# The second layer's output projection, all columns by seven block products, with the weight sums made in HBM

## The chip, the cores and the metric

One core of a Trainium2 chip. The metric is the device time of one launch in microseconds (us), as the median of runs; the kernel before has 2065.95 us (three runs, 2065.65 to 2066.11). TensorE is PE in the profile, VectorE DVE, ScalarE ACT, GpSimd POOL, SyncE SP. SP and POOL, and ACT for stores, issue the DMAs.

## The reference

A decoder trunk of two layers on x (1 x 512 x 2048, float32): a gated differential attention and a gated RWKV-7 time mixing. Each layer is a norm, a wide input projection, a mixer, a gate and an output projection that is added to x. The change concerns the last line of the second layer:

```
def rwkv7_mixer(h, ...):
    p = h @ w_in                          # 2048 -> 4*2048 + 192
    p = p + (token_shift(p) - p) * mu
    ...
    y = wkv7_scan(rh, heads(decay), kh, vh, -kk, kk * ah)     # 32 heads of 64, 512 tokens
    ...
    y = y.reshape(B, T, RW_WIDTH).astype(h.dtype) * jax.nn.silu(g)
    return y @ w_out                      # (512 x 2048) @ (2048 x 2048)

x = x + out
```

## The kernel before, in words

**Precision.** Every large matmul is made of three (`mm3`, L118): each float32 operand is split into a high and a low part, and high x high, high x low and low x high are summed in PSUM. The high part of a weight is a cast on ACT (L109), the low part a difference on DVE (L110), both in `split_w`. In the first layer's heads the same two stand at L615 and L616. A step is a stationary tile of 128 x 128 and 512 moving columns.

**Weights.** `w_out` lies as four column blocks of 512, each 16 K tiles of 128 rows. A load takes two K tiles (128 x 2 x 512 floats, 0.524 MB) from SP's queue into one of three buffers `wraw`; the split goes into four buffers `wh` and four `wl`, each one K tile.

**First layer.** Two dense units of 192 matmuls (`unit_tok`, 16 K tiles x 4 row tiles x 3), each with eight loads by L76 on SP, then seven heads by block products, whose weights are summed while loading: a second load of POOL's queue is added to a first one in SBUF (L588, `accum_op`).

**Second layer.** 16 rounds, one for each pair of heads. A round has four projections of 48 matmuls (`unit_chan`), with two loads each; a list of hooks (`behind`) hangs further work after the matmuls of certain K tiles. The scan of the pair before (`scan_pair`), cut into small steps, is spread between the matmuls. Each round's gated row of y (128 x 512) is stored to HBM (`yd2`). The last two rows stay in SBUF.

**The output projection** (end of `layer1`): the rows of y come back from HBM by `Feed` and are split (`split_row`). Column blocks 0 and 1 are dense units; the first runs beside the last scan, whose end is forced ahead of the last K tile (`all_rows`). Column blocks 2 and 3 go together through `seven`: the first 12 K tiles are two halves of 6, the 512 tokens two halves of 256, the 1024 columns two halves of 512. Seven block products, named 11, 12, 22, S1 to S4, stand for the eight; the last four K tiles are plain. A block product is 3 loads x 2 K tiles x 2 row tiles x 3 = 36 matmuls, a plain load 24. The sums of y (S1 to S4) are made by `sum_forms` on DVE and ACT during the second dense unit; the sums of the weights are added to blocks in SBUF by POOL (L790). Results are added to x by DVE (L827) and stored by ACT.

**What sets the order.** A scheduler orders each engine's instructions by priority and by their dependences. `issue_after(ins)` puts what it wraps behind `ins`, for the instructions on the engine of `ins`; `add_manual_dep` and priorities are the other means. Engines and DMA queues then run their instructions in the order built, each waiting on semaphores.

Of the kernel before, what the change touches and what calls it, by code (L numbers as in the profile page):

```python
# [13 lines left out]
F32 = mybir.dt.float32  # L14
F32R = mybir.dt.float32r
# [8 lines left out]
P = 128  # L24
# [56 lines left out]
class Halves:  # L81


    def __init__(self, parts, n):
        self.parts, self.n = parts, n
# [809 lines left out]
    return t[:].rearrange(f"p {n} -> p ({n})").rearrange("p (k c) -> p k c", k=KG)  # L895


def layer0(g, aps):
    nc, tc = g.nc, g.tc
    lx = ExitStack()  # L900
# [820 lines left out]
def layer1(g, aps):  # L1721
    nc, tc = g.nc, g.tc
    with ExitStack() as cx:
# [7 lines left out]
        def proj(i, j, **k):  # L1731
            return unit_chan(g, aps["rw_w_in"][i, j], P, **k)[0]
# [10 lines left out]
        def receptances(j):  # L1743
            def piece(f, i, p):
                def follow(m):
                    with tc.high_priority(offset=SCAN), tc.issue_after(m.ins):
                        f(g, i, p)
                return follow

            behind = [(39 if j == 1 else 39, lambda m: norms(g, j, pairs[j], m))]  # L1750
            if j:
                behind += [(27 if j > 1 else 45, lambda m: [mask_gram(g, pairs[j - 1], h, m) for h in range(2)]),
                           (18 if j == 1 else 12, piece(t_first, j - 1, pairs[j - 1])),
                           (39 if j == 1 else 33, piece(t_second, j - 1, pairs[j - 1]))]
            return shift_mix(g, proj(0, j, behind=behind), P, *mus(g, 0, j), "r", 1)

        begin(0)
        r = receptances(0)
        for j in range(D // P):
            p = pairs[j]  # L1760
            if j:
                others = [(1, lambda p=p: turn_keys(g, p, 0)), (2, lambda p=p: turn_keys(g, p, 4)),
                          (4, lambda p=p: turn_values(g, p))]
                if j > 1:
                    others.append((5 if j + 1 < D // P else 3, lambda i=j - 2: finish_y(g, i, pairs[i])))
                gaps = (6, 7) if j == 1 else (7, 8) if j < D // P - 1 else (5, 6)
                chain(g, j - 1, pairs[j - 1], 3 if j > 1 else 22, *gaps, others)
            ar = stage2(g, j, r, p)
            for q in pairs[j - 2 : j - 1] if j > 1 else ():
                q.now = True  # L1770
                if q.scale:
                    with tc.issue_after(ar.ins):
                        q.scale()
            p.now = j + 2 >= D // P

            def behind(m, j=j, p=p):
                if j > 1:
                    pairs[j - 2].chain.finish(g)
                with tc.issue_after(m.ins):
                    gram(g, j, p)  # L1780
                p.solve = Solve(g, t_solve(g, j, p))
            hooks = [(12 if 0 < j < LAG else 18, behind)]
            if j + 1 == D // P:
                hooks.append((39, lambda m, p=p: [mask_gram(g, p, h, m) for h in range(2)]))
            stage_v(g, j, p, proj(2, j, behind=hooks))
            turns = ()
            if j == 0:
                turns = ((9, lambda m: turn_keys(g, p, 0)), (15, lambda m: turn_keys(g, p, 4)),
                         (27, lambda m: turn_values(g, p)))
            if j + 1 < D // P:  # L1790
                begin(j + 1, turns)

            def finished(m, i=j - LAG):
                with tc.issue_after(m.ins):
                    gated(g, i, pairs[i], held)
                g.ys.extend((held, pairs[i].y))

            if j:
                gps = proj(3, j - 1, behind=[(36, finished)] if j >= LAG else ())
                held = gate(g, j - 1, gps, None)  # L1800
            if j + 1 < D // P:
                r = receptances(j + 1)
        chain(g, j, p, 3, 4, 5, whole=True)
        gts = [held, gate(g, j, proj(3, j), "E")]
        feed = Feed(g, g.yd2, KT - 2, lambda k: w.tile([P, T], F32, name="yr", bufs=1, tag=(
# [3 lines left out]
        def all_rows(n, m):  # L1809
            feed(n, m)  # L1810
            q = pairs[j - 1]
            if n >= 6 and not q.done:
# [4 lines left out]
            if n >= 8 and len(rows) == KT - 2:  # L1817
                rows.append(split_row(g, gts[0][:]))
            if n >= KT and len(rows) < KT:
                p.chain.finish(g)  # L1820
# [4 lines left out]
        sums = []  # L1825
# [5 lines left out]
        def all_sums(n, _):  # L1831
            if n >= 4 * len(sums) + 2 and len(sums) < NS // KG:
                if sums:
                    both = w.tile([P, 2, KG, 512], F32, name="frow", tag="G1", bufs=2)
                    frow = [both[:, i] for i in range(2)]
                else:
                    frow = [g.low.tile([P, KG, 512], F32, name="frow", tag=t, bufs=1)[:] for t in ("LT", "BK")]
                sums.append(sum_forms(g, g.yd2, len(sums), frow, homes))

        yH, yL = Rows(rows, 0), Rows(rows, 1)  # L1840
        for cb in range(2):
            cs = slice(cb * 512, (cb + 1) * 512)
            pts = unit_tok(g, yH, yL, aps["rw_w_out"][cb], 512, 2, more=(all_rows, all_sums)[cb],
                           late=cb == 0)
            for t in range(NT):
                if not cb:
                    xr = w.tile([P, 512], F32, name="xr1", tag=("r", "k", "th0", "th1")[t], bufs=1)
                elif t % 2 == 0:
                    xr = wide = g.low.tile([P, 2, 512], F32, name="xr1", tag="AR", bufs=3)
                xr = wide[:, t % 2, :] if cb else xr  # L1850
                nc.sync.dma_start(out=xr[:], in_=g.xd[t * P : (t + 1) * P, cs])
                nc.vector.tensor_add(xr[:], xr[:], pts[t][:])
                nc.scalar.dma_start(out=aps["out"][t * P : (t + 1) * P, cs], in_=xr[:])
        acc = {}
        for nm in ("11", "21", "22", "12"):
            t, c = PLACES[nm]
            a = g.low.tile([P, 2, 512], F32, name="acc", tag="AR", bufs=3)
            nc.sync.dma_start(out=a[:], in_=g.xd[t * 256 : t * 256 + 256, 1024 + c * 512 : 1536 + c * 512].rearrange(
                "(t p) c -> p t c", p=P))
            acc[nm] = [a[:, i, :] for i in range(2)]  # L1860

        def done(nm):
            t, c = PLACES[nm]
            for i, a in enumerate(acc[nm]):
                r0 = (2 * t + i) * P
                nc.scalar.dma_start(out=aps["out"][r0 : r0 + P, 1024 + c * 512 : 1536 + c * 512], in_=a)

        def banks(i):
            if i == 0:
                return [g.pp.tile([P, 512], F32, name="pp", tag="pp") for _ in range(2)]  # L1870
            return [g.ps.tile([P, 512], F32, name="pt", tag=("pb", "pc")[i - 1], bufs=2) for _ in range(2)]

        Ts = [flat(x) for x in g.TT] + [g.low.tile([P, KG, 512], F32, name="T2", tag="BK", bufs=1)]
        load = loader(g, aps["rw_w_out"], ((g.wraw, "wraw", 3), (w, "G1", 2), (g.wraw, "wraw", 3), (g.low, "LT", 1),
                                              (g.wraw, "wraw", 3), (w, "G1", 2)))
        seven(g, aps["rw_w_out"], load, rows, sums, 1024, 1536, acc, Ts, banks, done)


@with_exitstack
def body(ctx, tc, nc, aps):  # L1880
# [53 lines left out]
```

## Time and profile before

| | |
|---|---|
| runs, median (lowest to highest) | 2065.95 us (2065.65 to 2066.11) |
| the profiled execution | 2065.58 us |
| its span, first to last instruction | 2063.5 us |
| busy in the span: PE, DVE, ACT, POOL | 99%, 81%, 62%, 20% |
| HBM read, written | 251.41 MB, 15.99 MB |
| granted TensorE clock, mean | 1.000 |

The span leaves out what lies before the first and after the last instruction (2.1 us). Times in the views are us from the span's start. A row of instructions names the line, the engine, the operation, and out<-in tiles; in brackets stands the idle time ahead of it and what ended it. A row of DMA issues gives the size and the median time from issue to landing. TensorE's matmuls overlap, so their steps are read from the starts.

### The profile page before, as it was taken

Reading aid. Unit: us, or ns where it says so; the run is one execution under the profiler, and the core shown is the slowest. Engines: PE = TensorE matmul, PEld = TensorE weight load, DVE = VectorE, ACT = ScalarE, POOL = GpSimd, SP = SyncE. Lnnn points to the kernel's source line nnn. Section 1 sums busy time; section 2 is a strip of 40 time slices with the busy share of each in tenths; the row PEclk is TensorE's granted clock in tenths of the full one; section 3 lists DMA queues with packets and bytes.
Section 4 is the critical chain, followed back from the end, with each engine's and each line's share of the span. In section 5 each row is a group of like instructions: output and inputs, shape, how many; then the busy total and the mean of one; then the engine's idle time right before and its main releaser. Section 6 shows DMA issues by size and latency. Waiting matters only on the chain. (4 is left out here: it accounts for less than half of the span.)

```text
span 2063.5 us, 35254 instructions
## 1 busy us (share of the span) xinstructions
PE 2048.4 (99%) x11924; PEld 1689.0 (82%) x11924; DVE 1676.3 (81%) x4379; ACT 1276.0 (62%) x3043; POOL 417.8 (20%) x733
## 2 busy tenths in 40 slices
PE   9999999999999999999999999999999999999999
PEld 8878878888888888888778888888888888877887
DVE  5979798897978976576878888888888888887745
ACT  5667676776767754455666666666666666665433
POOL 0020211202111000101233322222333213232001
PEclk9999999999999999999999999999999999999999
DMA  6387877869688665742222222222222222244665
GB/s 203 114 166 184 167 169 167 179 172 177 172 161 217 171 200 187 179 114 95 75 75 70 82 77 81 76 87 75 78 76 80 70 89 74 84 134 151 214 165 121
DMA packets 100773, 269.70 MB, mean 131 GB/s; under 512 B 12432, under 2 KB 28960, under 8 KB 100592
## 3 DMA queue, kind: packets, MB, share of 16 engines
q1 hardware_dynamic: 62016, 173.21, 26.3%
q0 software_dynamic: 24144, 78.23, 20.8%
q10 hardware_dynamic: 14432, 16.01, 2.2%
q8 instruction: 94, 1.54, 0.3%
q14 instruction: 87, 0.71, 0.1%
HBM read 251.41 MB, written 15.99 MB: 130 GB/s over the span
## 5 line engine op out<-in xcount | busy, mean ns | idle before, releaser
L118 PE MATMUL pp<-hH,wh 128*128 128x512 f32 x1024 | 416.6, 407 | 0.0
L118 PE MATMUL pp<-hL,wh 128*128 128x512 f32 x1024 | 411.9, 402 | 0.0
L118 PE MATMUL pp<-hH,wl 128*128 128x512 f32 x1024 | 411.7, 402 | 0.0
L109 ACT CAST wh<-wraw 128x512 fp32r<-128x512 f32 (+1 forms) x412 | 254.3, 618 | 221.7 <-PE pp L118 128.8
L110 DVE TENSOR_TENSOR wl<-wraw,wh 128x512 fp32r<-128x512 f32 (+1 forms) x412 | 292.6, 711 | 83.2 <-ACT wh L109 77.7
L118 PE MATMUL pp<-wh,hH 128*128 128x512 f32 x820 | 325.1, 397 | 0.4 <-DVE G L382 0.4
L118 PE MATMUL pp<-wl,hH 128*128 128x512 f32 x820 | 321.8, 392 | 0.6 <-DVE wl L616 0.6
L118 PE MATMUL pp<-wh,hL 128*128 128x512 f32 x820 | 321.3, 392 | 0.0
L118 PEld LDWEIGHTS pp<-hH,wh 128*128 128x128 f32 x1024 | 192.8, 188 | 38.0 <-issue 2.1
L118 PEld LDWEIGHTS pp<-hH,wl 128*128 128x128 f32 x1024 | 193.1, 189 | 33.2
L118 PEld LDWEIGHTS pp<-hL,wh 128*128 128x128 f32 x1024 | 193.1, 189 | 31.4
L118 PE MATMUL pp<-wh,S 128*128 128x512 f32 x672 | 214.5, 394 | 0.0
L615 ACT CAST wh<-T 128x512 fp32r<-128x512 f32 x224 | 137.1, 621 | 94.2 <-PE pp L118 71.0
L118 PEld LDWEIGHTS pp<-wh,hH 128*128 128x128 f32 x820 | 154.0, 188 | 32.3 <-issue 0.6
L118 PEld LDWEIGHTS pp<-wh,hL 128*128 128x128 f32 x820 | 154.5, 188 | 31.4
L1633 POOL COPY SA<-VS 64x64 f32<-64x64 f32 x224 | 75.1, 335 | 518.2 <-DVE VS L1651 464.6
L118 PEld LDWEIGHTS pp<-wl,hH 128*128 128x128 f32 x820 | 154.2, 188 | 30.7 <-DVE wl L616 0.9
L616 DVE TENSOR_TENSOR wl<-T,wh 128x512 fp32r<-128x512 f32 x224 | 150.5, 686 | 25.4 <-ACT wh L615 24.8
L588 POOL DMA_DIRECT2D T<-in_da_w_in_dram x84 | 72.1, 858 | 388.5 <-DMA wraw<-in_da_w_in_dram 193.9
L1498 DVE SCALAR_TENSOR_TENSOR tmpl<-LT,n,Tm 128x60 f32<-128x60 f32 (+24 forms) x496 | 135.6, 273 | 13.3
L118 PEld LDWEIGHTS pp<-wh,S 128*128 128x128 f32 x672 | 124.7, 188 | 24.7 <-ACT wh L615 0.4
L118 PE MATMUL pp<-wl,S 128*128 128x512 f32 x336 | 132.2, 393 | 0.2 <-DVE wl L616 0.2
(377 smaller groups left out, 4015.3 us busy)
## 6 DMA issues: line engine op xcount, KB each, us to landing
wraw<-in_rw_w_in_dram SPq DMA_DIRECT2D x128, 512.0 KB, 3.6
T<-in_da_w_in_dram POOLq DMA_DIRECT2D x84, 512.0 KB, 6.4
wraw<-in_da_w_in_dram SPq DMA_DIRECT2D x64, 512.0 KB, 4.1
T<-in_da_w_in_dram SPq DMA_DIRECT2D x28, 512.0 KB, 4.4
wraw<-in_da_w_out_dram SPq DMA_DIRECT2D x26, 512.0 KB, 4.5
wraw<-in_rw_w_out_dram SPq DMA_DIRECT2D x26, 512.0 KB, 4.1
wraw<-in_da_w_in_dram POOLq DMA_DIRECT2D x21, 512.0 KB, 6.8
yr<-yd SPq DMA_DIRECT2D x22, 256.0 KB, 3.6
```

The costliest lines, as they stand in the source:

```text
L109: nc.scalar.copy(hi[:], raw[:, k : k + n])
L110: g.split = nc.vector.tensor_sub(lo[:], raw[:, k : k + n], hi[:].bitcast(F32)).ins
L118: m = nc.tensor.matmul(out, a, b, start=s, stop=e, skip_group_check=skip)
L588: self.g.nc.gpsimd.dma_start(out=raw, in_=src, accum_op=ALU.add)
L615: g.nc.scalar.copy(hi[:], raw[:, k])
L616: g.nc.vector.tensor_sub(lo[:], raw[:, k], hi[:].bitcast(F32))
L1498: st = nc.vector.scalar_tensor_tensor(tt, LT[:, i : i + 1, i + 1 :].to_broadcast([P, s, n]), n2[:, i : i + 1], Tm[:, 0:s, i : i + 1].to_br ...
L1633: nc.gpsimd.tensor_copy(p.SA[r_, c - 1, :], VS[r_, c, h, :])
```

## The change

All four column blocks of the second layer's output projection go through the seven products, as two pairs of blocks (`one` and `two`, each a `Blocks`). The halves of K are now tiles 8 to 13 and 0 to 5 (`FIRST`), and tiles 6, 7, 14 and 15 are plain (`PLAIN`). The sums of the y blocks are made once (`Forms`) and used by both pairs. The work starts with the products that need only early rows: 12 of both pairs, then 11 of both; after that `rest` for one pair and for the other.

The weight sums no longer come from adds in SBUF. `Sums` keeps four sums for each pair and each of three K groups, t1 to t4, in a tensor in HBM (`wsums`). Seven steps for each of the six groups make them: two copies, two adds, a copy t2 from t1, an add, a copy t3 from t2 and an add, copies on SP (L953) and adds on POOL (L956). A step is called from a hook in the rounds, wrapped in `issue_after(m.ins)` with a matmul `m`; what is left is called after the last round. All weights, sums too, come through one ring of buffers (`Ring`, loads by SP): three `wraw` and one of SX, later two more (`TT`, free after the scans).

The core of the diff:

```
+FIRST = {0: 8, 1: 0}
+PLAIN = (6, 14)
...
+class Sums:
...
+    def copy(self, out, src):
+        self.g.nc.sync.dma_start(out=out, in_=src)
+
+    def add(self, out, src):
+        self.g.nc.gpsimd.dma_start(out=out, in_=src, accum_op=ALU.add)
+
+    def plan(self):
+        for pair in range(2):
+            for i in range(NS // KG):
...
+                t1, t2, t3, t4 = [self.at[pair, n, i] for n in range(4)]
+                yield lambda: (self.copy(t1, b11), self.copy(t4, b22))
+                yield lambda: self.add(t1, b12)
+                yield lambda: self.add(t4, b12)
+                yield lambda: self.copy(t2, t1)
+                yield lambda: self.add(t2, b22)
+                yield lambda: self.copy(t3, t2)
+                yield lambda: self.add(t3, b21)
+
+    def step(self, m):
+        f = next(self.todo, None)
+        if f:
+            with self.g.tc.issue_after(m.ins):
+                f()
...
+def outputs_of(g, one, two, feed, finish, more):
...
+    N, s = NS // KG, 0
+    for i in range(N + 1):
+        for b in (one, two):
+            pace(s)
+            if i == N - 1 and b is two:
+                b.want("11")
+            b.first12(i)
+            s += KG
+    two.take("11", two.y)
+    for i in range(N):
...
+        one.first11(i)
...
+    for i in range(N):
+        two.first11(i)
+        if i == 1:
+            finish(None)
+            more(1)
+            one.sums.load(N - 1)
+    two.take("11", two.X)
+    one.sums.make("S1", g.m.ins)
+    one.rest(one.sums.make, finish)
+    two.rest()
...
-                           (39 if j == 1 else 33, piece(t_second, j - 1, pairs[j - 1]))]
+                           (39 if j == 1 else 33, piece(t_second, j - 1, pairs[j - 1])), (21, g.wsums.step)]
...
+        presum = [(21, g.wsums.step)]
...
-            stage_v(g, j, p, proj(2, j, behind=hooks))
+            stage_v(g, j, p, proj(2, j, behind=hooks + presum))
...
+        g.wsums.finish()
...
+        T2 = g.low.tile([P, KG, 512], F32, name="T2", tag="SX", bufs=3)
+        turn = lambda: g.wraw.tile([P, KG, 512], F32, name="wraw", tag="wraw")[:]
+        ring = Ring(g, [turn, turn, turn, lambda: T2[:]])
...
+        outputs_of(g, *two, all_rows, last_rows, lambda i: ring.homes.insert(1, lambda: flat(g.TT[i])))
...
+    g.wsums = Sums(g, dr, aps["rw_w_out"], "wsums")
```

How the built programs differ, on SP's queue in the first layer's two dense units, before. `wraw` from `da_w_in` are the weight loads, the last two of the first unit and the eight of the second; L590 loads for the first head:

```order
L275 DMA lq_682<-in_da_lam_q_dram 128x128
L276 DMA lk_683<-in_da_lam_k_dram 128x128
L979 DMA subw<-in_da_subln_w_dram 128x2x1
L76 DMA wraw<-in_da_w_in_dram 128x1024 x10
L590 DMA wraw<-in_da_w_in_dram 128x1024 x2
```

After, the first rows of the same place. `wsums` from `in_rw_w_out_dram` is a copy into a sum, `wsums` from `wsums` the copy of one sum into the next:

```order
L1233 DMA subw<-in_da_subln_w_dram 128x2x1
L953 DMA wsums<-in_rw_w_out_dram 128x1024
L76 DMA wraw<-in_da_w_in_dram 128x1024
L953 DMA wsums<-in_rw_w_out_dram 128x1024 x3
L76 DMA wraw<-in_da_w_in_dram 128x1024
L953 DMA wsums<-wsums 16x8192
L953 DMA wsums<-in_rw_w_out_dram 128x1024
L953 DMA wsums<-wsums 16x8192
L953 DMA wsums<-in_rw_w_out_dram 128x1024
L76 DMA wraw<-in_da_w_in_dram 128x1024
L953 DMA wsums<-wsums 16x8192 x3
L76 DMA wraw<-in_da_w_in_dram 128x1024
```

The 24 copies stand among these ten loads, the first ahead of the first and the last right ahead of the tenth.

POOL's queue before, from the mask of the attention on; L588 are the adds of the first layer's heads:

```order
masks.py:199 ISA
masks.py:199 AFFINE_SELECT ident<-ident 128x128
L984 AFFINE_SELECT mask<-mask 128x512
L588 DMA wraw<-in_da_w_in_dram 128x1024 x3
L588 DMA t_1291<-in_da_w_in_dram 128x512
```

After, the same place:

```order
masks.py:199 ISA
masks.py:199 AFFINE_SELECT ident<-ident 128x128
L1238 AFFINE_SELECT mask<-mask 128x512
L956 DMA wsums<-in_rw_w_out_dram 128x1024 x24
L588 DMA wraw<-in_da_w_in_dram 128x1024 x3
```

All 24 adds now stand ahead of the first add of the heads.

More of the change, by code (lines that the diff above doesn't have):

```diff
@@ new lines, with __init__, finish @@
+class Sums:
+    def __init__(self, g, dr, w, name):
+        self.g, self.w, self.steps = g, w, []
+        self.at = dr.tile([2, 4, NS // KG, P, KG, 512], F32, name=name)
+        self.todo = self.plan()
+    def copy(self, out, src):
[5 more added lines that the diff above has]
+            for i in range(NS // KG):
+                b11, b12, b21, b22 = [self.w[2 * pair + c, :, FIRST[kb] + i * KG : FIRST[kb] + (i + 1) * KG, :]
+                                      for kb in range(2) for c in range(2)]
+                t1, t2, t3, t4 = [self.at[pair, n, i] for n in range(4)]
[11 more added lines that the diff above has]
+                f()
+    def finish(self):
+        for f in self.todo:
+            f()
@@ new lines, in outputs_of, with pace @@
+def outputs_of(g, one, two, feed, finish, more):
+    def pace(n):
+        feed(4 + n // 2, g.m)
+    N, s = NS // KG, 0
[7 more added lines that the diff above has]
+    two.take("11", two.y)
+    for i in range(N):
+        pace(s)
+        pace(s + 1)
+        one.first11(i)
+        s += KG
+        if not i:
+            more(0)
+            one.want("11")
+            one.take("11", one.y)
+    one.take("11", one.X)
+    for i in range(N - 1):
+        one.sums.load(i)
+    for i in range(N):
+        two.first11(i)
[7 more added lines that the diff above has]
+    two.rest()
@@ L1798, in layer1 @@
             if j:
-                gps = proj(3, j - 1, behind=[(36, finished)] if j >= LAG else ())
+                gps = proj(3, j - 1, behind=[(36, finished)] * (j >= LAG) + presum)
                 held = gate(g, j - 1, gps, None)
@@ L1811, in all_rows @@
             q = pairs[j - 1]
-            if n >= 6 and not q.done:
+            if n >= 10 and not q.done:
                 q.chain.finish(g)
@@ L1816, in all_rows, with last_rows @@
                     gated(g, j - 1, q, gts[0], True)
[L1817 to L1820, printed above, removed]
+        def last_rows(whole):
+            if whole is not None:
+                return
+            rows.append(split_row(g, gts[0][:]))
+            p.chain.finish(g)
+            with tc.high_priority(offset=SCAN), tc.issue_after(g.m.ins):
                 finish_y(g, j, p)
@@ L1823, in all_rows @@
                 rows.append(split_row(g, gts[1][:]))
-        sums = []
         one = lambda *tags: [(g.low if t in LOW else w, t, {"y": 4}.get(t, LOW.get(t, 1))) for t in tags]
@@ L1829, in layer1 @@
                  {"S1": one("th0", "th1"), "S2": one("r", "k"), "S4": one("E", "thg"), "S3": one("yc", "v")})
[L1831 to L1875, printed above, removed]
@@ L1876, in layer1, with narrow, wide, sides @@
-        seven(g, aps["rw_w_out"], load, rows, sums, 1024, 1536, acc, Ts, banks, done)
+        def narrow():
+            return [g.low.tile([P, KG, 512], F32, name="frow", tag=t, bufs=1)[:] for t in ("LT", "BK")]
+        def wide():
+            both = w.tile([P, 2, KG, 512], F32, name="frow", tag="G1", bufs=2)
+            return [both[:, i] for i in range(2)]
+        sums = Forms(g, g.yd2, (narrow, wide, wide), homes)
+        def sides(c0, early):
+            acc = {}
+            def acc_of(nm):
+                if nm not in acc:
+                    t = early if nm == "11" else "AR"
+                    acc[nm] = g.low.tile([P, 2, 512], F32, name="acc", tag=t, bufs=3)
+                return [acc[nm][:, i, :] for i in range(2)]
+            def done(nm):
+                t, c = PLACES[nm]
+                for i, a in enumerate(acc_of(nm)):
+                    r0, c1 = (2 * t + i) * P, c0 + 512 * c
+                    nc.scalar.dma_start(out=aps["out"][r0 : r0 + P, c1 : c1 + 512], in_=a)
+            return acc_of, done
@@ new lines, in banks, with of @@
+        def banks(places):
+            def of(nm):
+                where = places[nm]
+                if where == "pp":
+                    return [g.pp.tile([P, 512], F32, name="pp", tag="pp") for _ in range(2)]
+                return [g.ps.tile([P, 512], F32, name="pt", tag=t, bufs=where.count(t)) for t in where]
+            return of
+        T2 = g.low.tile([P, KG, 512], F32, name="T2", tag="SX", bufs=3)
+        turn = lambda: g.wraw.tile([P, KG, 512], F32, name="wraw", tag="wraw")[:]
@@ new lines, in layer1 @@
+        ring = Ring(g, [turn, turn, turn, lambda: T2[:]])
+        two = []
+        for c0, at in ((0, {"f": ("pb", "pb"), "X": "pp", "y": ("pa", "pd"), "z": ("pc", "pc")}),
+                       (1024, {"f": "pp", "X": ("pb", "pb"), "y": "pp", "z": ("pc", "pc")})):
+            acc_of, done = sides(c0, "SX")
+            two.append(Blocks(g, aps["rw_w_out"], g.wsums.at, ring, rows, sums, c0 // 1024, g.xd, acc_of, banks(at),
+                              done))
+        outputs_of(g, *two, all_rows, last_rows, lambda i: ring.homes.insert(1, lambda: flat(g.TT[i])))
```

139 lines of the change are left out of this document (added).

## The prediction

> **What bounds the kernel now.** I read the page first: busy shares, then the DMA queues.
>
> ```profile
> PE 2048.4 (99%) x11924; PEld 1689.0 (82%) x11924; DVE 1676.3 (81%) x4379; ACT 1276.0 (62%) x3043; POOL 417.8 (20%) x733
> q1 hardware_dynamic: 62016, 173.21, 26.3%
> q0 software_dynamic: 24144, 78.23, 20.8%
> ```
>
> TensorE is busy for 99% of a span of 2063.5 us, so time is won only by fewer matmuls, and every wait of TensorE is paid in full. The two queue rows give the price of a transfer in the one thing that all queues share, the 16 DMA engines. q1 holds plain transfers: 26.3% of 2063.5 us, 542.7 us of all 16 engines, for 173.21 MB, so 319 GB/s and 1.64 us for 0.524 MB, the size of every weight block here. q0 holds mostly accumulating transfers (the adds issued from POOL): 429.2 us for 78.23 MB, 182 GB/s, 2.88 us a block.
>
> Next the chain of waits at the end, and the busy times by stage. The second column of the first view is us.
>
> ```profile
> 2021.22 8.25 PE pp L118 x36
> 2059.17 1.37 DVE acc L827 x2
> ```
>
> ```profile
> 25.00:50.00 25.00, 25.00 (x126) 20.61 (x125) 20.02 (x71) 17.73 (x40) 0.00 (x0) 1.00 0.33 93
> 50.00:75.00 25.00, 25.00 (x114) 20.74 (x113) 21.85 (x53) 20.41 (x64) 0.00 (x0) 1.00 0.32 102
> 75.00:97.00 22.00, 21.47 (x101) 17.48 (x100) 21.99 (x52) 12.11 (x28) 0.00 (x0) 1.00 0.36 111
> 97.00:150.00 53.00, 51.84 (x240) 41.55 (x239) 42.52 (x122) 34.82 (x77) 12.80 (x15) 1.00 0.87 175
> 2040.00:2063.50 23.50, 19.82 (x87) 15.90 (x85) 12.77 (x20) 6.21 (x10) 0.00 (x0) 0.96 0.18 68
> ```
>
> One product of 36 matmuls takes 8.25 us, 0.229 us each (the 0.39 us of a single one overlaps the next). From 25 to 97 us the DMA engines are about a third busy (third number from the right: granted clock, then DMA share, then GB/s); where adds run beside loads, from 97 on, they are at 0.87.
>
> **The change, part by part.**
>
> *Fewer matmuls.* Before, the projection takes 2 x 16 x 4 x 3 = 384 plus 7 x 36 + 4 x 24 = 348, in all 732; after, 2 x 348 = 696. That is 36 fewer, one product: -8.25 us.
>
> *The sums.* There are 24 copies within HBM on SP's queue and 24 adds on POOL's. The step is wrapped in an order after a matmul, but such an order binds only instructions of that matmul's own engine, TensorE, and these are SP's and POOL's. The built order shows what follows: all 48 stand at the front, in the first layer's second dense unit, and not in the rounds. TensorE, DVE and ACT keep their order until the output projection. So the question is what stands behind the 48.
>
> ```profile
> 24.01 0.43 SPq L979 DMA_DIRECT2D subw<-in_da_subln_w_dram  x1
> 25.32 52.07 SPq L76 DMA_DIRECT2D wraw<-in_da_w_in_dram  x10
> 82.62 6.09 SPq L590 DMA_DIRECT2D wraw<-in_da_w_in_dram  x2
> ```
>
> ```profile
> L76 SPq DMA_DIRECT2D wraw<-in_da_w_in_dram x10: 327/328/328, 25.3 to 77.1; - x10
> DMA to landing us min/median/max: 3.4/3.6/4.5
> ```
>
> ```profile
> 1.80 0.60 POOL L984 TENSOR_SCALAR_AFFINE_SELECT mask<-mask 128x512 bf16<-128x512 bf16 x1
> 100.95 1.00 POOL L588 DMA_DIRECT2D wraw<-in_da_w_in_dram  x1 [98.54 <-DVE wl L616]
> ```
>
> POOL is free from 2.4 to 100.95 us, so the adds can start as soon as the first copy has landed. On SP the first copy comes right before the first of the ten L76 loads, at 25.3 us, and the 24th right before the last, which was issued at 77.1 us. SP works in order, and 12 of the copies wait for an add on the block that they read. The last copy (t3 from t2 of the last group) waits for add 22. So the tenth load leaves SP only when 22 adds and 23 copies are done. When was that load needed?
>
> ```profile
> 90.05 0.62 ACT L109 CAST wh<-wraw 128x512 fp32r<-128x512 f32 x1
> 93.26 0.62 ACT L109 CAST wh<-wraw 128x512 fp32r<-128x512 f32 x1 [0.48 <-PE pp L118]
> 96.42 0.62 ACT L615 CAST wh<-wraw 128x512 fp32r<-128x512 f32 x1
> 99.17 0.63 ACT L615 CAST wh<-wraw 128x512 fp32r<-128x512 f32 x1 [1.60 <-PE pp L118]
> ```
>
> The casts at 90.05 and 93.26 are of that load (the last of L109). There are four buffers of casts, so the cast at 99.17 was released by the end of the half block ahead of the load's own, and its matmuls began at about 99.2. From issue to use it had 22 us of cover.
>
> Work for the DMA engines from 25.3 us until then: 22 adds at 2.88 (63.3) + 23 copies at 1.64 (37.8) + the nine loads at 1.64 (14.8) = 115.9 us. No row shows a copy or an add within HBM, so these are the prices of the nearest rows, a load into SBUF and an add into SBUF. The engines never stood at 1.0; I take the 0.87 of the window with adds: 115.9 / 0.87 = 133.2, so the load is issued at 158.5. It lands after some 6 us, with the last copy and the last adds beside it; the bounds are the 3.6 above and, at a crowded place, 8.4:
>
> ```profile
> T<-in_da_w_in_dram POOLq DMA_DIRECT2D x84, 512.0 KB, 6.4
> wraw<-in_da_w_in_dram SPq DMA_DIRECT2D x64, 512.0 KB, 4.1
> acc<-xd SPq DMA_DIRECT2D x4, 512.0 KB, 8.4
> ```
>
> ```profile
> L588 POOL DMA_DIRECT2D T<-in_da_w_in_dram x84 | 72.1, 858 | 388.5 <-DMA wraw<-in_da_w_in_dram 193.9
> ```
>
> Cast and difference take 0.62 and 0.69 us (rows above and below). The matmuls start at 165.8 instead of 99.2: **+66.6 us**. With the engines packed to 1.0 it is 49 us. If an add cost no more than a load (1.64), 35 us, and with that, full packing and a landing of 3.6, 20 us. If every copy and add took half as much again, 125 us; one after another, with 22 x (6.4 + 0.86 of issue) + 23 x 4.1 = 254 us, it would be 185. I stay with 66.6, since the adds' row already reads two streams for one written and the copies' row moves as many bytes, with the side above longer than the side below.
>
> The Trainium skill, "DMA: Bandwidth & Descriptors", section "Latency and other measured facts", gives copies between HBM tensors 214 GB/s at best, where q1 shows 319. By that a copy would cost 2.45 us, and the sum would grow by 23 x 0.81 / 0.87 = 21 us; no run so far shows such a copy.
>
> The waits by themselves cost nothing: five rounds of copy (4.1), issue (0.86) and add (6.4), one behind the other, are 57 us, and with the last three adds' issue the last load would leave at about 85 and be ready at 90, ahead of 99.2. It is the amount that decides. POOL's own next work, the L588 adds, began at 100.95, 24 us after that load was issued; by then adds 23 and 24 are in.
>
> While TensorE waits, it gets 24 matmuls (5.5 us) at a time, some 15 us apart (133.2 us over nine loads).
>
> The same skill, "TensorE: Matmul & The Clock Gate", Part 1, says that after an idle window of about 3.4 us the clock is halved until as long a busy one. The 0.96 of the window at the end, where TensorE is busy for only 19.82 of 23.5 us, agrees. By that the last group would lose 1.7 us more, and the clock row would dip in the stall.
>
> *The output projection.* It issues 48 loads where there were 29 and 12 adds: 78.7 us of the engines against 47.6 + 34.6 = 82.2, so no more; the adds there leave POOL's queue. Each load now feeds 12 matmuls from the start, and the first 14 stand in 168 matmuls (38.5 us) beside the last scan; before, about seven did.
>
> ```profile
> L110 DVE TENSOR_TENSOR wl<-wraw,wh 128x512 fp32r<-128x512 f32 x13 | 9.1, 699 | 1.7 <-ACT wh L109 1.6
> L476 DVE TENSOR_TENSOR hL<-yr,hH 128x512 fp32r<-128x512 f32 x10 | 6.9, 694 | 4.6 <-ACT hH L475 4.5
> ```
>
> ```profile
> 1885.00:1931.00 46.00, 45.92 (x277) 37.62 (x277) 29.85 (x72) 22.55 (x60) 11.76 (x23) 1.00 0.56 177
> ```
>
> DVE gets seven more loads to split there, 14 x 0.699 = 9.8 us, in the 46 us of this window, of which it was busy for 29.85, so 16 were free. I put **+3 us** for TensorE waiting for a split; bounds 0 and 9.8. The making of the four forms, one product ahead of its use, costs nothing: 3 x 4 x 1.4 us of DVE under 80 us of matmuls. The accumulators' loads that wait for a store on SP cost nothing either, with a ring of six blocks ahead. The end is as before: a sum from PSUM (1.37) and a store. Row 14 and the last scan's forced end move by a few matmuls and still stand ahead of tiles 14 and 15, so nothing.
>
> Sum against the profiled execution (2065.58 us, span 2063.5): 66.6 - 8.25 + 3 = +61.3, so 2126.9; the median of the runs, 2065.95, is 0.37 above it: **2127**.
>
> **The rivals.**
>
> *Faster after all.* The sums fit into idle DMA time, so that only the product and the 3 us are left: 2065.95 - 8.25 + 3 = 2060.7. For it: the share of 0.33 up to 97 us, and waits that fit. Against: to lose no more than is won, the load must leave SP by 99.5 us, so 74.2 x 0.87 = 64.6 us less 14.8 for nine loads, over 45 transfers: 1.1 us each, a third below the plain load's 1.64. Chance 0.05. The sums spread over the rounds, as the change's words say, would give the same time; the built order speaks against it. With a price near 1.3 it would come out within 0.2%: 0.03.
>
> *Adds as cheap as loads:* 35.5 - 8.25 + 3 = +30, 2096. For it: both read and write HBM, and an add's row may count waits of its own. Against: 182 and 319 GB/s. Chance 0.15.
>
> *Transfers within HBM are dearer by half:* 124.7 - 8.25 + 3 = +119.5, 2185. For it: reads and writes share one memory, and an add makes three streams of it; T's 6.4 against 4.1 us shows how much a second read costs. Against: no row. Chance 0.22.
>
> *The chance of the forecast* (stall of about 45 to 100 us, 2105 to 2160): 0.55.
>
> **How the numbers follow.** The range goes from 2080 (the cheapest sum above, 20 - 8.25, and a little) to 2190 (half as dear again), leaving out the faster case, the one without change and the far end of the dear one. About 0.2% is what a measurement here can tell from no change. Faster 0.05, same 0.03, slower 0.15 + 0.22 + 0.55 = 0.92.
>
> **What would show it.** In the changed profile: POOL's 24 L956 in one piece from about 29 us to 165; SP's L953 between the L76 loads; slices 2 to 4 of 40 with DMA at 8 or 9, TensorE well below 9 and a dip in its clock; L109's casts waiting for DMA for some 65 us in all, with the last at about 164; 36 matmuls fewer, and the distance from the last round to the end shorter by about 5 us. I am wrong if the L76 loads keep their times, if L953 and L956 lie in the rounds, or if the loss stands in the output projection.

## The result, and the profile after

| | before | after |
|---|---|---|
| median of four runs each | 2066.03 us | 2113.67 us |
| lowest to highest | 2065.65 to 2066.30 | 2111.68 to 2115.16 |
| ratio, 95% interval | | 1.023 (1.0212 to 1.0248) |
| profiled execution, its span | 2065.58, 2063.5 | 2111.68, 2109.9 |

The change makes the kernel 2.3% slower. The page of the changed kernel: busy shares, then three rows in 40 slices of 52.7 us (a digit is a share in tenths), then the two DMA queues.

```profile
PE 2054.1 (97%) x11888; PEld 1687.0 (80%) x11888; DVE 1697.5 (80%) x4417; ACT 1289.7 (61%) x3065; POOL 426.0 (20%) x739
...
PE   9579999999999999999999999999999999999999
...
PEclk9789999999999999999999999999999999999999
DMA  9999788796787956672212222222222222235664
...
q1 hardware_dynamic: 69136, 201.00, 29.8%
q0 software_dynamic: 25008, 81.38, 21.3%
```

There are 36 matmuls fewer, and nearly all that is lost stands in slices 2 and 3, about 53 to 158 us: TensorE at 5 and 7 tenths, its clock at 7 and 8, the DMA engines full. The same stretch as windows. Behind a window's length stand the busy times of PE, PEld (TensorE's weight loads), DVE, ACT and POOL; the last three numbers are the granted clock, the DMA share and GB/s. The profile's DMA share reads a little above 1 here:

```profile
25.00:50.00 25.00, 25.00 (x127) 20.72 (x125) 20.09 (x71) 17.81 (x39) 4.55 (x5) 1.00 0.94 267
50.00:75.00 25.00, 11.14 (x42) 8.26 (x40) 4.10 (x9) 5.39 (x15) 4.90 (x6) 0.78 1.02 262
75.00:100.00 25.00, 18.47 (x72) 14.78 (x72) 11.74 (x30) 7.58 (x22) 4.11 (x5) 0.84 1.04 288
100.00:131.50 31.50, 17.99 (x55) 12.55 (x55) 16.20 (x40) 10.45 (x34) 5.75 (x7) 0.72 1.05 267
```

SP's queue there. L953 are the copies, L76 the weight loads (the third, fourth, eighth and tenth of ten are shown); a copy that reads a sum (`wsums<-wsums`) waits for an add ahead of it:

```profile
24.71 0.60 SPq L953 DMA_DIRECT2D wsums<-in_rw_w_out_dram  x1
...
48.86 0.54 SPq L76 DMA_DIRECT2D wraw<-in_da_w_in_dram  x1
57.32 8.40 SPq L953 DMA_DIRECT2D wsums<-wsums  x3
65.81 0.53 SPq L76 DMA_DIRECT2D wraw<-in_da_w_in_dram  x1
...
116.12 0.52 SPq L76 DMA_DIRECT2D wraw<-in_da_w_in_dram  x1
...
130.89 0.47 SPq L953 DMA_DIRECT2D wsums<-wsums  x1
131.45 0.53 SPq L76 DMA_DIRECT2D wraw<-in_da_w_in_dram  x1
```

The tenth load, which left SP at 77.1 before, leaves at 131.45. POOL's adds, by line (first and last start behind the durations), are the one piece at the front that was forecast, and end 30 us earlier:

```profile
L956 POOL DMA_DIRECT2D wsums<-in_rw_w_out_dram x24: 805/818/1082, 31.2 to 135.8; - x24
```

Now TensorE's waits over 1 us in the stretch, from the timeline, and the cast of the first head that answers to the one at 99.17 before:

```profile
63.21 0.80 PE L118 MATMUL pp<-wh,hH 128*128 128x512 f32 x1 [6.97 <-ACT hH L1427]
...
76.97 0.79 PE L118 MATMUL pp<-wh,hH 128*128 128x512 f32 x1 [8.87 <-ACT t L336]
...
101.70 0.79 PE L118 MATMUL pp<-wh,hH 128*128 128x512 f32 x1 [6.26 <-ACT wh L109]
...
126.08 0.80 PE L118 MATMUL pp<-wh,hH 128*128 128x512 f32 x1 [8.60 <-ACT wh L109]
134.97 0.48 PE L361 MATMUL pt<-ident,t 128*128 128x128 f32 x1 [6.09 <-ACT t L328]
```

```profile
148.04 0.63 ACT L615 CAST wh<-wraw 128x512 fp32r<-128x512 f32 x1 [1.60 <-PE pp L118]
```

148.04 - 99.17 = 48.9 us is the stall. TensorE's waits are 36.8 us of it; most of the rest is TensorE at half clock behind each wait (below). Four of the five waits, 30.7 us, go back to a cast that a weight load held: two releasers are such casts, and two (hH, t L336) stand in ACT's queue behind one. The last wait is of another kind: t L328 waits for VectorE's work, not for a load. ACT's casts themselves waited for loads six times from 30 to 148 us, 49.6 us in all:

```profile
ACT wh L109 <- DMA wraw<-in_da_w_in_dram: 49.6, 6, 12.3
```

To place later gains and losses I use two landmarks that all kernels have, the first and last group of `gp` matmuls in the rounds. Before and after:

```profile
964.41 1.83 PE L1405 MATMUL gp<-AR,BK 64*128 64x128 f32 x28
1838.00 2.06 PE L1405 MATMUL gp<-AR,BK 64*128 64x128 f32 x32
```

```profile
1012.25 1.94 PE L1659 MATMUL gp<-AR,BK 64*128 64x128 f32 x30
1885.41 1.83 PE L1659 MATMUL gp<-AR,BK 64*128 64x128 f32 x28
```

From the last one to the end of the span it is 225.5 us before and 224.5 after: the output projection, with 36 matmuls fewer, is worth 1.0 us.

### The profile page after: what moved, and what is told of

The parts are those of the page before. It is cut to its first block, busy times and chain, and to the rows that moved or that the text cites. A ratio compares the mean times of both kernels' runs of the same rounds, so it can differ in the third digit from the quotient of the medians.

```text
span 2109.9 us, 35368 instructions
## 1 busy us (share of the span) xinstructions
PE 2054.1 (97%) x11888; PEld 1687.0 (80%) x11888; DVE 1697.5 (80%) x4417; ACT 1289.7 (61%) x3065; POOL 426.0 (20%) x739
## 3 DMA queue, kind: packets, MB, share of 16 engines
q1 hardware_dynamic: 69136, 201.00, 29.8%
q0 software_dynamic: 25008, 81.38, 21.3%
## 5 line engine op out<-in xcount | busy, mean ns | idle before, releaser
L118 PE MATMUL pp<-hH,wh 128*128 128x512 f32 x1024 | 416.6, 407 | 0.0
L118 PE MATMUL pp<-hL,wh 128*128 128x512 f32 x1024 | 411.9, 402 | 0.0
L118 PE MATMUL pp<-hH,wl 128*128 128x512 f32 x1024 | 411.7, 402 | 0.0
L118 PE MATMUL pp<-wh,hH 128*128 128x512 f32 x784 | 315.9, 403 | 31.8 <-ACT wh L109 15.2
L118 PE MATMUL pp<-wl,hH 128*128 128x512 f32 x784 | 311.9, 398 | 0.8 <-DVE wl L616 0.6
L118 PE MATMUL pp<-wh,hL 128*128 128x512 f32 x784 | 310.6, 396 | 0.0
L118 PEld LDWEIGHTS pp<-hH,wh 128*128 128x128 f32 x1024 | 192.8, 188 | 37.9 <-issue 2.1
L118 PEld LDWEIGHTS pp<-hH,wl 128*128 128x128 f32 x1024 | 193.1, 189 | 33.2
L118 PEld LDWEIGHTS pp<-hL,wh 128*128 128x128 f32 x1024 | 193.2, 189 | 31.4
L118 PE MATMUL pp<-wh,S 128*128 128x512 f32 x672 | 214.4, 394 | 0.0
L118 PEld LDWEIGHTS pp<-wh,hH 128*128 128x128 f32 x784 | 149.7, 191 | 65.0 <-ACT wh L109 16.5
L615 ACT CAST wh<-T 128x512 fp32r<-128x512 f32 x224 | 137.3, 621 | 92.8 <-PE pp L118 71.7
L118 PEld LDWEIGHTS pp<-wl,hH 128*128 128x128 f32 x784 | 149.7, 191 | 31.3 <-DVE wl L110 1.7
L118 PEld LDWEIGHTS pp<-wh,hL 128*128 128x128 f32 x784 | 149.9, 191 | 30.9 <-DVE hL L1428 0.5
L588 POOL DMA_DIRECT2D T<-in_da_w_in_dram x84 | 72.2, 860 | 385.8 <-DMA wraw<-in_da_w_in_dram 155.1
L118 PEld LDWEIGHTS pp<-wh,S 128*128 128x128 f32 x672 | 124.7, 188 | 24.3
L118 PE MATMUL pp<-wl,S 128*128 128x512 f32 x336 | 132.0, 393 | 0.0
```

Of the source, the lines that this page charges most:

```text
L118: m = nc.tensor.matmul(out, a, b, start=s, stop=e, skip_group_check=skip)
L588: self.g.nc.gpsimd.dma_start(out=raw, in_=src, accum_op=ALU.add)
L615: g.nc.scalar.copy(hi[:], raw[:, k])
```

## The experiments

All eight, with the profiled execution cut at the landmarks. "Stall" is the start of the cast of L615 (L618 in e7) less 99.17 us. The median of the kernel before was 2065.70 us beside the first four and 2065.07 beside the last four.

| kernel | time, us | stall | to first `gp` | rounds | last `gp` to end |
|---|---|---|---|---|---|
| before | 2066.03 | 0 | 964.4 | 873.6 | 225.5 |
| after | 2113.67 | 48.9 | 1012.3 | 873.2 | 224.5 |
| e1_held | 2065.55 | 0.1 | 964.5 | 874.9 | 224.7 |
| e2_eighth (one run) | 2074.36 | 11.4 | 974.5 | 873.3 | 224.3 |
| e3_breadth (one run) | 2107.51 | 46.6 | 1008.2 | 873.1 | 224.4 |
| e4_no_sums | 2063.88 | 0.2 | 962.8 | 873.6 | 224.0 |
| e5_half (one run) | 2084.13 | 18.9 | 983.4 | 873.9 | 224.8 |
| e6_shared | 2063.63 | 0.7 | 963.3 | 875.1 | 222.2 |
| e7_pool | 2068.87 | 0.7 | 967.0 | 874.8 | 227.4 |
| e8_late | 2061.90 | 0.3 | 962.4 | 874.6 | 221.2 |

The columns come from one profiled execution each. The part up to the first `gp` lies anywhere from 962.4 to 967.0 us in the five kernels without the stall, so gains of 1 to 3 us are read from the other columns as well as from the ratio. Five kernels with the same projection (after, e1, e2, e3, e5) lie within 0.5 us of each other in the last column.

**e1_held: the sums truly in the rounds.** Each transfer gets, beside the step's order after a matmul, a pin behind the instruction traced before it on its own queue.

```
-        self.g.nc.sync.dma_start(out=out, in_=src)
+        self.g.tc.keep_in_program_order(self.g.nc.sync.dma_start(out=out, in_=src))
...
-        self.g.nc.gpsimd.dma_start(out=out, in_=src, accum_op=ALU.add)
+        self.g.tc.keep_in_program_order(self.g.nc.gpsimd.dma_start(out=out, in_=src, accum_op=ALU.add))
```

Expected: 

> All 48 transfers keep their bytes, but each is pinned behind the instruction traced before it on its own queue, so that copies and adds lie in the second layer's rounds. Theory (the loss is the amount of work in front of the tenth weight load): the 48.9 us of the first layer's dense unit go away and nothing takes their place, since the page shows DMA at 0.2 in the rounds; 2113.7 - 48.9 = 2064.8 us, within 2. Rival (the sums cost wherever they stand, by POOL's waits for copies or by contention in HBM): 2070 us or more, with new waits of TensorE in the rounds. Rival (the output projection alone is worth the full 8.25 - 3): 2060.7.

Measured: 2065.55 us, ratio 0.9999 (0.9990 to 1.0008). The window from 50 to 75 us is that of before again:

```profile
50.00:75.00 25.00, 25.00 (x114) 20.71 (x112) 21.85 (x53) 20.40 (x64) 0.00 (x0) 1.00 0.33 103
```

So the whole loss belongs to the place of the 48 transfers; the rest of the change comes to nothing. In the rounds they cost 1.3 us (874.9 against 873.6 in e4, without sums, and before), against none expected.

**e2_eighth: the amount taken away, the waits kept.**

```
-        self.g.nc.gpsimd.dma_start(out=out, in_=src, accum_op=ALU.add)
+        self.g.nc.gpsimd.dma_start(out=out[:16], in_=src[:16], accum_op=ALU.add)
```

Expected: 

> Each add covers only 16 of the 128 partitions of its block, an eighth of the bytes (so the sums, and the result, are not the reference's); number, order and waits of all copies, adds and loads stay. Theory (amount): work ahead of the tenth load falls from 22 x 2.7 + 23 x 1.6 + 9 x 1.6 = 110.6 us to 22 x 0.34 + 36.8 + 14.4 = 58.7 us of the DMA engines; the tenth load leaves SP at about 84 to 92 and the stall is 0 to 8 us; 2065 to 2073 us. Rival (waits in SP's order): most of the stall stays, 30 us or more, 2095 us or more.

Measured: one run, 2074.36 us, a stall of 11.4 us, a little above the theory's range and far below the rival's. SP's tenth load, then TensorE's two waits over 1 us:

```profile
92.57 0.53 SPq L76 DMA_DIRECT2D wraw<-in_da_w_in_dram  x1
```

```profile
82.16 0.50 PE L118 MATMUL pp<-wh,hH 128*128 128x512 f32 x1 [1.21 <-ACT wh L109]
...
96.70 0.48 PE L361 MATMUL pt<-ident,t 128*128 128x128 f32 x1 [6.84 <-ACT t L328]
```

The amount is most of the loss, but 92.57 is a time at which, by the prediction, next to nothing should be lost: with its 6 us to land and 1.3 for cast and difference that makes 99.9, against 99.2. And TensorE waits longest for t L328, which VectorE prepares, not for a load.

**e3_breadth: the waits covered, the amount kept.** `plan` does each of the seven steps for all six groups before the next step.

```
+        for todo in (lambda t, b: (self.copy(t[0], b[0]), self.copy(t[3], b[3])),
+                     lambda t, b: self.add(t[0], b[1]), lambda t, b: self.add(t[3], b[1]),
...
+            for t, b in rows:
+                yield lambda: todo(t, b)
```

Expected: 

> The same 48 transfers at the same front, but the plan goes over all six groups at each step instead of one group after the other, so that a copy that needs an add comes six or more transfers behind it. Theory (amount): 23 copies, nine loads and by then 18 to 22 adds stand ahead of the tenth load as before, 100 to 111 us of the engines; tenth load at 125 to 136 and a stall of 42 to 54 us; 2107 to 2119 us. Rival (waits in SP's order): the waits are covered, and the stall falls under 25 us; 2090 us or less.

Measured: one run, 2107.51 us, a stall of 46.6. SP's last two loads:

```profile
117.91 1.01 SPq L76 DMA_DIRECT2D wraw<-in_da_w_in_dram  x2
```

Covering SP's waits for adds gained 2.3 us of the stall. Together with e2: mostly the amount, not the order within the group. But the tenth load left 13 us earlier than in the changed kernel, and the stall shrank by 2.3 only, so the tenth load is not what counts.

**What counts instead.** VectorE's splits of those loads, grouped by line, in after, e3, e2 and before, each from 30 us to the end of its stall (148, 148, 112 and 100 us). Behind the second bar stands VectorE's idle time ahead of the 22 splits, then the part of it that a cast ended:

```profile
L110 DVE TENSOR_TENSOR wl<-wraw,wh 128x512 fp32r<-128x512 f32 x22 | 15.1, 689 | 50.9 <-ACT wh L109 50.8
```

```profile
L110 DVE TENSOR_TENSOR wl<-wraw,wh 128x512 fp32r<-128x512 f32 x22 | 15.1, 691 | 48.0 <-ACT wh L109 47.8
```

```profile
L110 DVE TENSOR_TENSOR wl<-wraw,wh 128x512 fp32r<-128x512 f32 x22 | 15.1, 690 | 13.5 <-ACT wh L109 13.4
```

```profile
L110 DVE TENSOR_TENSOR wl<-wraw,wh 128x512 fp32r<-128x512 f32 x22 | 15.0, 685 | 3.0 <-ACT wh L109 3.0
```

Against before, this idle time grew by 47.9, 45.0 and 10.5 us, and the stalls are 48.9, 46.6 and 11.4. The sizes alone prove little: the same work in a stretch that is longer by the stall leaves that much more idle time. What counts is the place: all of the growth stands behind casts, and the casts waited for loads (49.6, 47.2 and 11.6 us of ACT's time).

VectorE had little slack: it was busy for 21.99 of 22.00 us from 75 to 97 before, and for 21.85 of 25.00 ahead of that. It prepares the heads there (S, rope, norms) in one queue with the splits, so a load that is late for its split pushes all of that back, even if it is early enough for its matmuls, and TensorE meets it as a wait for t L328: 6.1, 9.4 and 6.8 us in after, e3 and e2, against 0.5 before. In e2 this is all but 1.2 us of TensorE's waits over 1 us, so there the path through VectorE is seen by itself. In after and e3 TensorE waits longer for late casts than for t L328; it was as full as VectorE before (25.00 of 25.00 us up to 75), and how much of those stalls each path makes is not told apart.

**e5_half: every load against the tenth alone.** The first pair's sums stay at the front, the second pair's are pinned (`self.held` decides).

```
+    def pin(self, ins):
+        if self.held:
+            self.g.tc.keep_in_program_order(ins)
...
+                self.held = pair > 0
```

Expected: 

> The first pair's three groups of sums (12 copies, 12 adds) stay at the front, the second pair's are pinned in the rounds. By the prediction's own sum (only the tenth load counts, with 22 us of cover): 12 x 1.6 + 11 x 2.7 + 9 x 1.6 = 63 us of the engines, tenth load out at about 88, no stall; about 2066 us. Theory now (each load counts as it comes, since VectorE is full there and what it waits for a split is lost): the third and fourth loads stand behind as much work as in the changed kernel, which had lost 21 us by the fourth; a stall of 15 to 22 us and no more after it; 2080 to 2088 us; VectorE's idle time ahead of the splits of the first 100 us grows by as much as the time.

Measured: one run, 2084.13 us, a stall of 18.9. SP's fourth load and the last six, and the splits (to 118 us):

```profile
64.91 0.53 SPq L76 DMA_DIRECT2D wraw<-in_da_w_in_dram  x1
77.18 19.12 SPq L76 DMA_DIRECT2D wraw<-in_da_w_in_dram  x6
```

```profile
L110 DVE TENSOR_TENSOR wl<-wraw,wh 128x512 fp32r<-128x512 f32 x22 | 15.0, 686 | 21.8 <-ACT wh L109 21.7
```

Half the amount, which by the prediction's own sum cost nothing, costs 18.9 us, and VectorE's idle time grew by 18.8. From the fifth on nothing is ahead of the loads any more, and the stall doesn't grow; but what was lost by then doesn't come back. So each load counts as it comes, and not the tenth alone. Of VectorE's path e5 says little: TensorE's waits over 1 us are two, 5.2 and 9.5 us, behind the held casts of the third and fourth load, and t L328 costs 0.7.

**e4_no_sums: the output projection alone.**

```
-            raw = self.ring(self.wsums[self.pair, {"S1": 0, "S2": 1, "S3": 3}[nm], i])
+            raw = self.raw(0, FIRST[0] + i * KG)
...
-        f = next(self.todo, None)
+        f = None
```

Expected: 

> No copies and no adds at all; the output projection loads plain blocks of w_out where it loaded sums (so the result is not the reference's), the same number of loads of the same size. Theory: the output projection alone, 2064.8 us, within 1, a gain of about 1 us on the kernel before; its chain of waits shows the same split wait (1.3) and scan waits as the changed kernel. The difference to the kernel with the sums held in the rounds is what the sums cost there: 0 to 1 us. Rival (some of the output projection's lost gain comes from sums read back from HBM): 2061 to 2063.

Measured: 2063.88 us, ratio 0.9990 (0.9981 to 0.9999); 1.5 us less than before from the last `gp` to the end. The projection gains little by itself; reading sums back is worth at most 0.7 of what it lost. What is left of the loss lies within the projection, beside the last scan. Three windows of 20 us each from its first matmul, before, then after:

```profile
1883.00:1903.00 20.00, 19.93 (x129) 15.88 (x128) 14.65 (x37) 12.19 (x33) 5.21 (x12) 1.00 0.48 157
1903.00:1923.00 20.00, 20.00 (x150) 16.42 (x149) 11.82 (x29) 10.07 (x27) 6.55 (x12) 1.00 0.64 196
1923.00:1943.00 20.00, 20.00 (x92) 16.55 (x91) 16.83 (x35) 8.25 (x15) 0.00 (x0) 1.00 0.64 210
```

```profile
1930.00:1950.00 20.00, 19.18 (x118) 13.77 (x117) 16.30 (x40) 14.98 (x37) 5.57 (x9) 1.00 0.64 190
1950.00:1970.00 20.00, 19.58 (x147) 15.19 (x147) 17.28 (x35) 12.44 (x32) 6.20 (x11) 1.00 0.54 163
1970.00:1990.00 20.00, 18.13 (x81) 14.41 (x80) 17.63 (x40) 9.04 (x16) 0.00 (x0) 1.00 0.72 245
```

TensorE idles 3.0 us more (59.93 busy before, 56.89 after), VectorE has 7.9 us more to do. Taken over all starts of L118 in the projection, what the steps take beyond TensorE's own pace (0.228 us a matmul) sums to 10.1 us before and 15.9 after. The largest single wait in after, and what VectorE waited for ahead of it:

```profile
1977.63 0.50 PE L118 MATMUL pt<-wl,hH 128*128 128x512 f32 x1 [1.33 <-DVE wl L110]
```

```profile
1974.86 0.69 DVE L924 TENSOR_TENSOR frow<-frow 128x512 f32<-128x512 f32 x1 [2.20 <-DMA frow<-yd]
```

L924 makes the first form of y (`Forms.make`). It is wrapped in an order after `g.m.ins`, a matmul, and so is not bound on VectorE either: the first of its three operations runs at 1933.38, early in the last scan, and the second, shown here, stands ahead of splits and waits for rows whose loads leave SP only at 1967.60 and 1968.03, with the scan's last matmuls.

**e6_shared: fewer splits beside the last scan.**

```
+        same = nm == "12" and self.pair
+        raw = None if same else self.raw(0, k0) if nm != "22" else self.ring(self.wsums[self.pair, 2, i])
...
+        wt = Blocks.kept if same else split_w(self.g, None, KG, 512, 0, self.raw(c, k0))
```

Expected: 

> Sums held in the rounds, and the second pair's first four block loads and their eight splits left out: its 12 products use the first pair's split weights (so the result is not the reference's). All matmuls stay. Theory (the output projection lost its gain because VectorE and ACT have twice as many splits beside the last scan): TensorE's small waits around the scan's steps (10.9 us over the matmuls' own pace, against 7.2 in the kernel before) fall to about 8; 2061.5 to 2063.5 us, 2 to 4 less than with the sums held. Rival (the waits come from where the scan's steps stand among the matmuls): within 1 us of the held one, 2065.5.

Measured: 2063.63 us, ratio 0.9994 (0.9985 to 1.0003), so not to be told from before, and between the theory's range and the rival's; 2.5 us less than e1 from the last `gp` to the end. The waits around the scan's steps fell from 10.9 us in e1 to 10.0 and not to 8; part of the rest is a shorter wait for L924's rows (TensorE's wait on wl is 0.79 instead of 1.62 us). By an estimate from these, eight splits fewer explain one or two us, not the six.

**e7_pool: splits moved to POOL.**

```
+            if low and k:
+                low.tensor_sub(lo[:], raw[:, k : k + n], hi[:].bitcast(F32))
...
+        low = self.g.nc.gpsimd if nm == "12" or nm == "11" else None
```

Expected: 

> Sums held in the rounds, and in the products 12 and 11 of both pairs the low part of every second K tile is made by POOL instead of VectorE: 12 differences of 128x512, 8.2 us of VectorE beside the last scan. The reference is computed. Theory (VectorE's splits delay the scan's steps): 2062 to 2064 us. Rival (POOL takes longer for a difference, and its own scan copies wait behind it): 2066 to 2069 us.

Measured: 2068.87 us, ratio 1.0022 (1.0012 to 1.0032), the rival's time. POOL's largest group beside the scan:

```profile
L111 POOL TENSOR_TENSOR wl<-wraw,wh 128x512 fp32r<-128x512 f32 x9 | 14.4, 1597 | 17.2 <-ACT wh L109 13.5 <-PE px L1805 3.8
```

A difference takes 1.6 us there on average, against 0.69 on VectorE, so the rival's first half holds. Its second half is not shown: POOL's 9.7 us of idle time ahead of the scan's copies (L1891) are nearly all put down to VectorE.

**e8_late: the first form behind the plain block's split.** The order is now after `g.split`, which is an instruction of VectorE.

```
         self.plain(PLAIN[0], 0, (z, 256, True, False))
+        then("S1", self.g.split)
         finish(False)
...
-    one.sums.make("S1", g.m.ins)
```

Expected: 

> Sums held in the rounds, and the first form of y is made behind the split of the plain block that comes after the products 11, and not ahead of it. The order it had before was tied to a matmul, which does not bind VectorE. Theory: VectorE no longer waits 2.5 us for the third pair of rows ahead of a split, so TensorE's wait of 1.6 us goes, and the first group's three operations leave the start of the last scan: 2063 to 2064.5 us. Rival (the forms come too late for the S1 products): 2066 us or more, with waits of TensorE for fS.

Measured: 2061.90 us, ratio 0.9985 (0.9976 to 0.9995), 0.15% faster than the kernel before and below the theory's range. From the last `gp` to the end it is 221.2 us, 3.5 less than e1. The third window of the projection:

```profile
1922.00:1942.00 20.00, 20.00 (x91) 16.55 (x91) 19.27 (x42) 9.66 (x17) 0.00 (x0) 1.00 0.84 290
```

TensorE's wait there is gone, with VectorE busier than before (19.27 of 20).

## Why the prediction was right, and where not

**The cause was right, the path in part.** The 48 transfers stood at the front, since the order after a matmul did not hold SP's and POOL's instructions; SP's queue held the loads behind them; the DMA engines were full; TensorE starved. e1 shows it: pinned in the rounds, the 48 cost 1.3 us instead of 48.9. 2113.67 us lies in the forecast's own 2105 to 2160, 13 below its 2127: a stall 18 us shorter and a gain in the projection 4 us smaller than forecast.

**The stall, 48.9 instead of 66.6: the packing.** The sum divided the engines' work by 0.87, the share of a window with adds. The windows show 0.94 to 1.05. With 1.0, which the prediction gave as a bound, the same sum is 49. The casts waited for loads for 49.6 us, where the forecast had some 65, and the last of them at 125.41 instead of about 164. The prices were near: the queue rows with and without sums (29.8% of 2109.9 us against 28.8% of 2060.4 in e4 for q1, 21.3% against 18.6% for q0) give 1.47 us of all engines a copy and 2.76 an add, where 1.64 and 2.88 were used. This takes it that all other transfers cost the same in both, and the rows' last digit is worth 0.1 us a transfer. The rows of e4, then of e1:

```profile
q1 hardware_dynamic: 67024, 188.41, 28.8%
q0 software_dynamic: 21552, 68.79, 18.6%
```

```profile
q1 hardware_dynamic: 69136, 201.00, 30.7%
q0 software_dynamic: 25008, 81.38, 22.3%
```

**That 49 agrees so well is partly luck.** The step that failed is "from issue to use it had 22 us of cover", with the tenth load as the one that counts. The tenth load's cast did not wait for it; the last cast that waited for a load was one of the eighth, issued at 116.12:

```profile
125.41 1.14 ACT L109 CAST wh<-wraw 128x512 fp32r<-128x512 f32 x2 [11.79 <-DMA wraw<-in_da_w_in_dram]
```

A load's first users are the cast and, behind it, VectorE's split, and VectorE, which the quoted row had at 21.99 of 22.00, had no time to spare there. Nor did the sum count the loads ahead of the tenth. e5, where the prediction's sum gives no stall, measured 18.9, and e2 11.4 with the tenth load out at 92.57. "The amount decides" held (e2, e3); "the waits by themselves cost nothing" did not quite: covering them gained 2.3 us in e3, and e2 lost 11.4 us with the DMA engines at 0.82 to 0.84 from 25 to 100 us, not full.

**The rivals on price** fall with the queue rows: neither were adds as cheap as loads, nor transfers within HBM dearer by half. The Trainium skill, "DMA: Bandwidth & Descriptors", section "Latency and other measured facts", would have had 2.45 us a copy by its 214 GB/s; 1.47 us of engine time here, and 1.68 in e1 by its 30.7%, disagree, and the mixed transfers of the windows moved 262 to 288 GB/s, so that term of 21 us was rightly left out. No run here times copies alone.

**The clock** dipped as forecast, but to 0.72 to 0.84 over the whole stretch, not in the last group alone. After each wait some 4 to 14 matmuls start 0.43 us or more apart instead of 0.23; after the first:

```profile
63.80 0.63 PE L118 MATMUL pp<-wl,hH 128*128 128x512 f32 x1
64.23 0.63 PE L118 MATMUL pp<-wh,hL 128*128 128x512 f32 x1
...
67.48 0.39 PE L118 MATMUL pp<-wl,hH 128*128 128x512 f32 x1
67.71 0.40 PE L118 MATMUL pp<-wh,hL 128*128 128x512 f32 x1
```

Over the five waits that sums to some 11 of the 48.9 us (1.3 to 3.4 us each); where TensorE then waits for the next load anyway, it costs nothing by itself. The Trainium skill, "TensorE: Matmul & The Clock Gate", Part 1, has half the clock until about 3.4 us of sustained work; the some 4 us from 63.21 to 67.21 agree.

**The output projection, -1.0 instead of -5.25.** The 36 matmuls went (about -8), but TensorE's steps beyond its pace grew by 5.9 us, and the way from the start of the last sums to the span's end by 0.8 (from 4.3 to 5.1 us). The term "+3 us for a split", with bounds 0 and 9.8, was the right kind and too small; and that the making of the four forms costs nothing was wrong: e8, which moves only the first of them, gives 3.5 us back. I had seen that an order after a matmul doesn't bind DMAs, and did not ask it of the same wrapping around VectorE's work.

**What stays open.** How the stall of the changed kernel divides between loads late for TensorE and loads late for VectorE, and how e2's 11.4 us divide between the amount that was left and SP's order, was not measured. The 1.3 us of the sums in the rounds grow in small steps from round to round and were not traced to one wait. Of the 5.9 us in the projection, e6 and e8 explain some 4.5 between them (an estimate, 1 and 3.5) if their parts don't overlap, which wasn't tried.

## What to carry to other kernels

Before you trust an order between instructions, look on which engines it binds; here the same mistake put 48 transfers in front of ten loads (48.9 us) and a sum in front of a scan (3.5 us). Count the cover of every load, not only of the last, and count it up to its first user: here VectorE and TensorE were both full, and what a load was late for its cast was lost (18.9 us in e5, by the third and fourth load), also where it was still early for TensorE (e2). Transfers that cost 1.3 us in a stage with idle DMA engines cost 48.9 in another: the place decides, so look at the built order first.

## What the runs showed of the hardware

By the queue rows with and without them, copies between HBM tensors of 0.524 MB took 1.47 us (after) to 1.68 us (e1) of the 16 DMA engines, about as much as loads into SBUF (1.64), and adds within HBM 2.76 us beside the first layer (3.21 in the rounds, by 22.3% of 2064.1 us in e1 against e4). The engines' share came to 0.94 to 1.05 at 262 to 288 GB/s for over 100 us, where I had taken 0.87. A difference of 128x512 took POOL 1.6 us on average in e7, 2.3 times VectorE's 0.69.
